# Opening order, state-pass buffers and the engine of the block differences in a hybrid convolution and mLSTM layer

## The chip, the core and the metric

The kernel runs on one core of a Trainium2 chip. The metric is device time in microseconds (us) of one execution. Engines are named as in the profile: PE (TensorE matmul), PEld (TensorE weight load), DVE (VectorE), ACT (ScalarE), POOL (GpSimd), SP (SyncE). SP issues nearly all DMA transfers, in order, so a transfer that has to wait holds those behind it.

## The reference, cut to what matters

One layer with 2048 latent tokens of 1024 channels and 256 context tokens, all in float32:

```python
shift, scale, gate = split(silu(c) @ w_ada + b_ada, 3)
hx = rmsnorm(x, g_norm) * (1 + scale) + shift           # 2048 x 1024
px = hx @ w_in + b_in                                    # 1024 -> 11296 columns
pc = hc @ w_in[:, :STATE_COLS] + b_in[:STATE_COLS]       # context: q, k, v and gates alone
_, ctx_states = mlstm_bidir(pc, (zero_state, zero_state), emit=False)
h_x, _ = mlstm_bidir(px[..., :STATE_COLS], ctx_states, emit=True)
y_a = b_a * dwconv3(c_a * x_a) * silu(z_a)
y_b = sigmoid(o) * headnorm(h_x) * silu(z_b)
merged = sigmoid(g_a) * (y_a @ w_pa) + sigmoid(g_b) * (y_b @ w_pb)
out = rmsnorm(x + gate * (merged @ w_out + b_out), g_final)
```

`mlstm_scan` steps over chunks of tokens. Each chunk's state is `C_new = decay * C + k^T (wk * v)`, together with a running sum n and a running maximum m. It is run forward and backward, from the final context state of that direction.

## The kernel before

**Matmuls.** Each float32 operand is split into a rounded part ("hi", a cast on ACT, L178) and a remainder ("lo", a subtraction on DVE, L179), and each product is three matmul passes (hi hi, hi lo, lo hi). The input projection works on pairs of 128-column blocks and two halves of 512 tokens with a scheme of seven block products in place of eight. `Stream` makes the seven weight operands from raw tiles. Their sums are formed on POOL (`total`, L345), and then split. `Operands` holds the seven token operands. PE's instructions run in the order in which the program writes them. The other engines' instructions are ordered by a scheduler, except those wrapped in `pin`, which keep program order on their engine.

**Halves.** The sequence is worked in two halves of 1024 tokens (`T`): A first, then B. Beside the dense matmuls, generators in two queues, `urgent` and `later`, put smaller work between PE's instructions. `run(dense, rate, urate)` takes a step of `later` after each 1/rate matmuls, and `gap(n)` is n steps of nothing.

**Opening.** The 1024 tokens of half A are loaded as eight tiles of 128 rows (`load_rows`), their squares are summed on ACT (L199), the scale is formed in three small steps on POOL (L200, L186, L187), and the rows are scaled on DVE (L205); together that is `norm`. The modulation vectors come from 16 tiles of `w_ada`, in four quarters kk of four tiles (`load_ada`). `ada(kk)` multiplies them on PE (L1045), `modulation(kk)` turns the result into `gsc` and `shift` on DVE (L1052 to L1054). `turned(kk, ns)` transposes four row tiles into a PSUM bank (L212) and applies the modulation (L216 on ACT, L217 on DVE). `cut_first` and `cut_sums` make the seven token operands of that quarter: differences on DVE (`less`, L1083), then the split. `mms(kk)` does the first four products of the quarter (L1062). The `w_ada` tiles lie in places that token operands take over later: the remainder tiles of the third quarter's operands 5 and 6 are those of the last modulation quarter.

**State pass.** The scan over chunks needs the state ahead of each chunk, in both directions. `state_scan` runs one direction in advance: for each pair of chunks it loads a tile of tokens (`tk`, from `tokd`, L702), weights v on POOL (`weigh`, vw, L631), multiplies k by it on PE (L636), updates the state on DVE (L640) and stores the states of both chunks back into `tokd` (L739). `load` runs one item ahead, with two `tk` buffers. `ctx_scan` does the same for the context. In half A it runs beside the dense products of `w_in`, in half B once for each pair of heads, between the dense products and the full `scan`, which uses the tags `tk`, `qk` and `mw` with two buffers each.

**Block differences.** While half A's products run, `prep_b` normalises and transposes half B's tokens into `xod`, and `late_rows` forms the gate row and multiplies `w_out` by it (L1295) into `wod`. `combine` then loads blocks of each and makes the four differences that the seven products need (L295), in place, and stores them. All these elementwise operations are on POOL. The input tiles are in a pool tag of four buffers (`big`).

Of the kernel before, what the change touches and what calls it, by code (L numbers as in the profile page):

```python
# [41 lines left out]
def hybrid_kernel(ctx: ExitStack, tc, x, c, ctxt, c_ctx, w_ada, b_ada, g_norm, w_in, b_in,  # L42
# [236 lines left out]
    def combine(src, tile):  # L279

        bs = {}

        def load(kk):
            if kk < 4:
                bs[kk] = [tile([P, 2, NB]) for _ in range(2)]
                for n, t in enumerate(bs[kk]):
                    ld.dma_start(t, src[2 * n:2 * n + 2, :, kk, :].rearrange("o p i -> p o i"))

        load(0)
        yield from gap(10)  # L290
        for kk in range(4):
            load(kk + 1)
            (b11, b12), (b21, b22) = [(t[:, 0, :], t[:, 1, :]) for t in bs[kk]]
            for d, a, b in ((b11, b12, b11), (b12, b22, b12), (b22, b22, b11), (b21, b21, b22)):
                pin(nc.gpsimd.tensor_tensor(d, a, b, op=OP.subtract))  # L295
                yield from gap(2)
            yield from gap(2)
            for n, t in enumerate(bs.pop(kk)):
                ld.dma_start(src[4 + 2 * n:6 + 2 * n, :, kk, :].rearrange("o p i -> p o i"), t)
            yield from gap(4)  # L300
# [352 lines left out]
        nc.scalar.copy(tok[:, :, 0:P], pt[:, 0:n * P].rearrange("p (c d) -> p c d", d=P))  # L653
        ld.dma_start(dst, tok)

    def tok_tile(pool):
        return pool.tile([P, 2, P + 258], F32, tag="tk", name=nm("tk"), bufs=2)

    def ctx_scan(pool):
        tks = {}  # L660

        def load(h):
            if h < NH:
                tks[h] = tok_tile(pool)
                ld.dma_start(tks[h][:, :, 0:P + 129], tcd[h])

        load(0)
        yield from gap(8)
        for h in range(NH):
            load(h + 1)  # L670
            tk = tks.pop(h)
            for d in (1, 0):
                g = gt["C"][d]
                order = (0, 1) if d == 0 else (1, 0)
                js = [h * 2 + c for c in order]
                vws = [weigh(tk[:, c], g["wk"][:, j:j + 1]) for c, j in zip(order, js)]
                yield from gap(2)
                mid, fin = cstate(), cstate()
                update(mid, None, tk[:, order[0]], vws[0], None, "pn")
                yield  # L680
                update(fin, mid, tk[:, order[1]], vws[1], g["dec"][:, js[1]:js[1] + 1], "pn")
                yield
                ld.dma_start(cini[h] if d == 0 else std[1][h], fin)

    def state_scan(pool, heads, half):

        d = 0 if half == 0 else 1
        g = gt["AB"[half]][d]
# [9 lines left out]
        def load(m):  # L698
            if m < len(items):
                h, p, _, c0 = spot(2 * m)  # L700
                tks[m] = tok_tile(pool)
                ld.dma_start(tks[m][:, :, 0:P + 129], tokd[half][h, :, c0:c0 + 2, 0:P + 129])  # L702
# [8 lines left out]
                vws[n] = weigh(tks[n // 2][:, ch - c0], g["wk"][:, j:j + 1])  # L711

        load(0)
        yield from gap(8)
        ready(0)
        yield from gap(2)
        for n in range(2 * len(items)):
            h, p, ch, c0 = spot(n)
            if n % 2 == 0:
                load(n // 2 + 1)  # L720
            else:
                yield
            tk = tks[n // 2]
# [287 lines left out]
              (1, 0), (1, 1), (0, 0), (0, 1), (5, 0), (5, 1), (6, 0), (6, 1)]  # L1011
    adas = {}

    def load_ada(kk):

        for n, m in enumerate((kk, kk + 4, NK + kk, NK + kk + 4)):
            o, p = PLACES[4 * kk + n]
            adas[kk, n] = xslot(4 * o + 2 * p + 1, [P, NK, P])
            ld.dma_start(adas[kk, n], w_ada.rearrange("(k p) n -> p k n", p=P)[:, :, m * P:(m + 1) * P])

    st = Stream((t[0] for t in todo), (0, 2, 1, 3, 4, 5, 6))
    load_rows(0, 4)
    load_ada(0)
    load_rows(4, 8)
    load_ada(1)
    st.begin()
    load_ada(2)
    load_ada(3)
# [8 lines left out]
    gsc = cp.tile([P, NK, 2], F32, name="gsc")  # L1037
    padas = {}

    def ada(kk):  # L1040

        pada = padas[kk] = pu_ps().rearrange("p (n a s) -> p n a s", n=4, s=2)
        for n in range(4):
            for k in range(NK):
                nc.tensor.matmul(pada[:, n], adas[kk, n][:, k, :], sc[:, k, None, :].to_broadcast([P, 64, 2]),  # L1045
                                 start=(k == 0), stop=(k == NK - 1))

    def modulation(kk):
# [13 lines left out]
            nc.tensor.matmul(ps[b], ops[o][wi][:, kk, :], xA.at(o, xi, kk), start=(not more and kk + pi == 0),  # L1062
                             stop=(kk == 3 and pi == 2), skip_group_check=True)

    def turned(kk, ns):

        for n in ns:
            pt = bank(n)
            turn(pt, rows[4 * (n // 2):4 * (n // 2) + 4], kk + 4 * (n % 2))
            v = vs[kk, n] = vslot() if n < 2 else t2k()  # L1070
            pin(modulate(v, pt, kk + 4 * (n % 2), 0, nc.scalar if n < 3 else None))

    def cut(kk, o, v):
        if kk % 2 == 0:
# [26 lines left out]
        for a in todo:  # L1101
            cut(*a)

    def mms(kk):
        for o, b in EARLY_OPS:
            mm(o, b, kk)

    EARLY_OPS = ((0, "X"), (2, "U"), (3, "W"), (1, "Y"))
    st.pinned = True
    ada(0)  # L1110
    normed(0, 4)
    transposed_rows()
    modulation(0)
    turned(0, (0, 1))
    cut_first(0)
    normed(4, 8)
    turned(0, (2, 3))
    ada(1)
    rest(cut_sums(0))
    modulation(1)  # L1120
    turned(1, range(4))
    cut_first(1)
    st.fill(2)
    more = cut_sums(1)
    st.fill(4)
# [2 lines left out]
    ps.update((b, dense_ps()) for _, b in EARLY_OPS)  # L1128
    ada(2)
    modulation(2)  # L1130
    turned(2, range(4))
    mms(0)
    cut_first(2)
    more = cut_sums(2)
    ada(3)
    modulation(3)
    rest(more)
    turned(3, range(4))
    mms(1)
    mms(2)  # L1140
    cut_first(3)
    rest(cut_sums(3))
    mms(3)
    s1, u2, u3 = uslot(), uslot(), uslot()
    nc.scalar.copy(s1, ps["X"])
    fin(0, 0, ps["U"], s1)
    nc.vector.tensor_tensor(u2, ps["Y"], s1, op=OP.add)
    nc.vector.tensor_tensor(u3, ps["W"], u2, op=OP.add)
    for n, (o, b) in enumerate(((4, "Z"), (5, "V"), (6, "Z"))):
        ops[o] = st.take(n + 1)  # L1150
        if o < 6:
# [95 lines left out]
    def late_rows():  # L1247
# [44 lines left out]
        for k in range(NK):  # L1292
            load(out_rows, k + 1)
            wr = wrs.pop(k)
            pin(nc.gpsimd.tensor_tensor(wr, wr, gate_t, op=OP.mult))  # L1295
# [4 lines left out]

    later.extend([prep_b(), late_rows()])
    later.append(ctx_scan(sb))
    later.append(state_scan(sb, range(NH), 0))
    for item, fin, w in todo[kv_end:]:
        run(pair(st, xA, fin), 0.235, 0.5)
    flush(urgent)
# [17 lines left out]
    EARLY = 3  # L1324
    kinds = half_fins(1)
    heads = [f"k{r} v{r} q{r} o{r} z{r} X{r} C{r} Z{r} B{r}" for r in range(4)]
    todo = plan(kinds, " ".join(heads) + " a0 a1 a2 a3 b0 b1 b2 b3")
    st = Stream(t[0] for t in todo)
    for item, fin, w in todo:
# [4 lines left out]
        if w[0] == "z":  # L1334
            flush(urgent)
            hs = 2 * r, 2 * r + 1
            later.extend([state_scan(sp_, hs, 1), scan(sp_, hs, 1)])
            if r < EARLY:
                later.append(scan(sp_, [r], 0))
    flush(urgent)  # L1340
# [204 lines left out]
```

## Time and profile before

| | |
|---|---|
| time, median of 3 runs | 2711.37 us (2708.78 to 2716.03) |
| the profiled execution | 2719.64 us, span 2717.9 us |
| PE busy | 2613.6 us, 96% of the span |
| DVE, ACT, POOL busy | 1717.8, 1063.4, 1216.7 us |
| mean granted TensorE clock | 0.988 |
| DMA | 458.10 MB, mean 169 GB/s |

A row of the timeline has the start, the duration, the engine, the source line, the operation, output <- input by tile names, partitions x elements, and a count; the bracket is the idle time of the engine ahead of it and what ended that. "SPq" rows are the DMA issues. In lists of waits the columns are total, number of times and longest. In tables of stretches the columns are the stretch, its length, the busy time of PE, PEld, DVE, ACT and POOL with their instruction counts, then the granted clock, the mean busy share of the DMA engines, and GB/s.

### The profile page before, as it was taken

What the parts mean: (1) busy time and instruction counts of PE and PEld (TensorE: products, weight loads), DVE (VectorE), ACT (ScalarE), POOL (GpSimd) and SP (SyncE); (2) the same over time, 40 slices, a digit from 0 to 9 for tenths busy, and PEclk for the clock granted to TensorE, in tenths of its full rate; (3) what the DMA queues carried; (4) which work ended last, traced back from release to release, by engine and by line L of the source; (5) the groups of instructions that cost most, each with busy time, mean ns of one, the idle gap of its engine ahead of it and who ended that gap; (6) DMA issues with size and microseconds to landing.
All of it is one profiled execution on the core that took longest, in us unless ns stands there. A gap on an engine that the chain in (4) does not pass through costs nothing.

```text
span 2717.9 us, 38189 instructions
## 1 busy us (share of the span) xinstructions
PE 2613.6 (96%) x12807; PEld 2176.6 (80%) x12807; DVE 1717.8 (63%) x3075; ACT 1063.4 (39%) x2168; POOL 1216.7 (45%) x1411
## 2 busy tenths in 40 slices
PE   5999999999999999999999999999999999899998
PEld 5788887787778787877887888788888888788776
DVE  4642338888876657477577577667656655444686
ACT  4433334333343335343443444344444433222332
POOL 2212123544665543235555565465555335433464
PEclk8999999999999999999999999999999999999999
DMA  7323343555633567434644654654556978868542
GB/s 218 92 93 106 104 138 119 176 162 159 213 124 103 171 180 240 118 104 144 196 151 122 183 165 133 180 172 126 168 180 211 301 246 258 267 196 280 201 147 93
DMA packets 370082, 458.10 MB, mean 169 GB/s; under 512 B 23853, under 2 KB 268253, under 8 KB 369885
## 3 DMA queue, kind: packets, MB, share of 16 engines
q1 hardware_dynamic: 369648, 455.57, 54.3%
q8 instruction: 102, 1.67, 0.3%
q14 instruction: 96, 0.78, 0.1%
q10 hardware_dynamic: 236, 0.08, 0.0%
HBM read 324.60 MB, written 130.97 MB: 168 GB/s over the span
## 4 chain that ended last, share of the span: by engine, by line
PE 62%; DVE 7%; DMA 5%; issue 3%; POOL 2%; ACT 1%; SPq 0%; POOLq 0%; DVEq 0%; ACTq 0%
PE pd L412 43%; PE pd L459 11%; PE pn L841 2%; PE pn L842 2%; DVE wl L179 2%; DMA tokd<-tk 1%; PE pn L636 1%; DMA tk<-tokd 1%; PE pa L793 1%; PE pu L636 1%; DVE xt L1467 1%; DVE cv L946 1%; DMA x<-xod 1%; DVE t2k L873 1%; DMA xt<-in_x_dram 1%
## 5 line engine op out<-in xcount | busy, mean ns | idle before, releaser
L412 PE MATMUL pd<-x,wh 128*128 128x512 f32 x5320 | 1702.5, 398 | 27.9 <-DVE t2k L873 14.7
L412 PEld LDWEIGHTS pd<-x,wh 128*128 128x128 f32 x5320 | 988.9, 190 | 224.7 <-issue 28.6
L412 PE MATMUL pd<-x,wl 128*128 128x512 f32 x2660 | 1060.9, 399 | 0.0
L412 PEld LDWEIGHTS pd<-x,wl 128*128 128x128 f32 x2660 | 503.8, 189 | 100.2 <-issue 0.2
L179 DVE TENSOR_TENSOR wl<-sw,wh 128x512 fp32r<-128x512 f32 x384 | 314.1, 819 | 195.1 <-ACT wh L178 188.8
L178 ACT CAST wh<-sw 128x512 fp32r<-128x512 f32 x384 | 238.2, 620 | 504.4 <-PE pd L412 426.8
L178 ACT CAST wh<-wr 128x512 fp32r<-128x512 f32 x352 | 217.8, 619 | 403.6 <-PE pd L412 260.4
L179 DVE TENSOR_TENSOR wl<-wr,wh 128x512 fp32r<-128x512 f32 x352 | 299.3, 851 | 44.3 <-ACT wh L178 43.4
L345 POOL TENSOR_TENSOR sw<-wr,sw 128x512 f32<-128x512 f32 x96 | 134.0, 1396 | 395.4 <-DVE wl L179 327.7
L631 POOL TENSOR_SCALAR vw<-tk,wk 128x129 f32<-128x129 f32 x272 | 200.0, 743 | 209.4 <-DMA tk<-tokd 153.5
L459 PE MATMUL pd<-x,wh 128*128 128x512 f32 x896 | 283.1, 398 | 0.0
L345 POOL TENSOR_TENSOR sw<-wr 128x512 f32<-128x512 f32 x96 | 130.2, 1356 | 196.6 <-DVE wl L179 187.1
L459 PEld LDWEIGHTS pd<-x,wh 128*128 128x128 f32 x896 | 167.3, 189 | 32.5
L459 PE MATMUL pd<-x,wl 128*128 128x512 f32 x448 | 174.4, 399 | 0.0
L345 POOL TENSOR_TENSOR sw<-sw,wr 128x512 f32<-128x512 f32 x96 | 135.3, 1409 | 74.5 <-DVE wl L179 62.9
L854 ACT ACTIVATE hf<-pn,rd 128x128 f32<-128x128 f32 x128 | 47.0, 368 | 275.1 <-DVE rd L850 256.5
L779 POOL TENSOR_SCALAR_AFFINE_SELECT mw<-mw 128x256 f32<-128x256 f32 x128 | 64.3, 523 | 200.2 <-DMA mw<-mwd 168.3
L873 DVE TENSOR_TENSOR t2k<-pd,u 128x512 f32<-128x512 f32 x168 | 115.4, 687 | 59.4 <-PE pd L412 58.6
L345 POOL TENSOR_TENSOR sw<-wr,wr 128x512 f32<-128x512 f32 x96 | 137.4, 1431 | 18.5 <-DMA wr<-in_w_in_dram 12.4
L186 POOL TENSOR_SCALAR ssq<-ssq 128x1 f32<-128x1 f32 x128 | 36.9, 288 | 186.5 <-ACT hf L856 180.6
L841 PE MATMUL pn<-tk,pt 128*128 128x129 f32 x512 | 99.5, 276 | 3.1 <-DVE hb L855 3.1
L880 DVE SCALAR_TENSOR_TENSOR t2k<-pd,cols,u 128x512 f32<-128x512 f32 x73 | 54.7, 750 | 74.0 <-PE pd L412 68.0
(236 smaller groups left out, 3331.6 us busy)
## 6 DMA issues: line engine op xcount, KB each, us to landing
wr<-in_w_in_dram SPq DMA_DIRECT2D x176, 512.0 KB, 4.2
mw<-mwd SPq DMA_DIRECT2D x64, 512.0 KB, 5.1
tk<-tokd SPq DMA_DIRECT2D x64, 386.0 KB, 4.2
tk<-tokd SPq DMA_DIRECT2D x64, 257.0 KB, 3.0
qkd<-t2k SPq DMA_DIRECT2D x64, 256.0 KB, 2.9
qk<-qkd SPq DMA_DIRECT2D x64, 256.0 KB, 3.9
tokd<-t2k SPq DMA_DIRECT2D x32, 258.0 KB, 3.0
tokd<-tk SPq DMA_DIRECT2D x64, 129.0 KB, 3.4
```

What stands on the lines that cost most here:

```text
L178: a = nc.scalar.copy(hi, raw)
L179: b = (eng or nc.vector).tensor_tensor(lo, raw, hi.bitcast(F32), op=OP.subtract)
L345: nc.gpsimd.tensor_tensor(s, a, b, op=op)
L412: nc.tensor.matmul(ps[b], op[wi][:, kk, :], xs.at(o, xi, kk), start=(fresh and kk + pi == 0), stop=(o == last[b] and kk == 3 and pi == 2), ...
L459: nc.tensor.matmul(pss[j], ops[k // 4][wi][:, k % 4, :], y(xi, k, j), start=(k + pi == 0), stop=(k == NK - 1 and pi == 2))
L631: pin(nc.gpsimd.tensor_scalar(vw, tk[:, VT], wk, None, op0=OP.mult))
L636: nc.tensor.matmul(pu, tk[:, KT], vw, start=True, stop=True)
L779: pin(nc.gpsimd.affine_select(mws[m][:, :, 0, d, :], mws[m][:, :, 0, d, :], pattern=[[0, 2], [s, P]], base=0, channel_multiplier=-s, compa ...
L841: nc.tensor.matmul(pn[:, d, :], pt[:, d, :], tk[:, VT], start=True, stop=False)
L842: nc.tensor.matmul(pn[:, d, :], qw[:, d, :], cur if d == carried else tk[:, ST], start=False, stop=True)
L873: nc.vector.tensor_tensor(t, ps, add, op=OP.add)
L880: nc.vector.scalar_tensor_tensor(dst, ps, bcol(col), add, op0=OP.add, op1=OP.add)
```

## The change

1. Loads: the first modulation quarter comes ahead of all x rows; the second quarter's first two tiles come between the two groups of four rows, and its other two behind them.
2. Opening order: the first two modulation tiles are multiplied ahead of everything else; the squares and scaling of rows 4 and 5 move ahead of the first transposes' modulation, those of rows 6 and 7 behind the first split. The modulation of the first two transposed tiles is done on DVE, all others on ACT. From the second quarter on, parts of the early products and of the transposes alternate; `rest(more)` of the third quarter comes ahead of the last `modulation`; the fifth operator's weights are taken ahead of the first evacuation.
3. State pass: four buffers in place of two, loads two items ahead. In half B the odd items use the `mw` buffers. The context pass gets four buffers.
4. The differences in `combine` and the product of `w_out` with the gate are on DVE.

```diff
@@ combine
-                pin(nc.gpsimd.tensor_tensor(d, a, b, op=OP.subtract))
+                pin(nc.vector.tensor_tensor(d, a, b, op=OP.subtract))
@@ late_rows
-            pin(nc.gpsimd.tensor_tensor(wr, wr, gate_t, op=OP.mult))
+            pin(nc.vector.tensor_tensor(wr, wr, gate_t, op=OP.mult))
@@ state pass
-    def tok_tile(pool):
-        return pool.tile([P, 2, P + 258], F32, tag="tk", name=nm("tk"), bufs=2)
+    def tok_tile(pool, bufs=2):
+        return pool.tile([P, 2, P + 258], F32, tag="tk", name=nm("tk"), bufs=bufs)
...
-                tks[h] = tok_tile(pool)
+                tks[h] = tok_tile(pool, 4)
...
-                tks[m] = tok_tile(pool)
+                tks[m] = tok(m)
...
         load(0)
+        load(1)
         yield from gap(8)
...
-                load(n // 2 + 1)
+                load(n // 2 + 2)
...
-    later.append(state_scan(sb, range(NH), 0))
+    later.append(state_scan(sb, range(NH), 0, lambda m: tok_tile(sb, 4)))
...
+    def tok_b(m):
+        if m % 2 == 0:
+            return tok_tile(sp_)
+        t = sp_.tile([P, NK, P], F32, tag="mw", name=nm("tm"), bufs=2)
+        return t.rearrange("p k n -> p (k n)")[:, 0:2 * (P + 258)].rearrange("p (c n) -> p c n", c=2)
...
-            later.extend([state_scan(sp_, hs, 1), scan(sp_, hs, 1)])
+            later.extend([state_scan(sp_, hs, 1, tok_b), scan(sp_, hs, 1)])
@@ loads
+    load_ada(0)
     load_rows(0, 4)
-    load_ada(0)
+    load_ada(1, (0, 1))
     load_rows(4, 8)
-    load_ada(1)
+    load_ada(1, (2, 3))
@@ turned
-            pin(modulate(v, pt, kk + 4 * (n % 2), 0, nc.scalar if n < 3 else None))
+            pin(modulate(v, pt, kk + 4 * (n % 2), 0, eng))      # eng=nc.scalar by default
@@ opening
-    ada(0)
+    ada(0, (0, 1))
+    transposed_rows()
     normed(0, 4)
-    transposed_rows()
+    ada(0, (2, 3))
     modulation(0)
-    turned(0, (0, 1))
+    normed(4, 6)
+    turned(0, (0, 1), None)
     cut_first(0)
-    normed(4, 8)
+    normed(6, 8)
+    ada(1, (0, 1))
     turned(0, (2, 3))
-    ada(1)
+    ada(1, (2, 3))
     rest(cut_sums(0))
     modulation(1)
-    turned(1, range(4))
+    turned(1, (0, 1))
     cut_first(1)
+    turned(1, (2, 3))
     st.fill(2)
...
     ada(2)
     modulation(2)
-    turned(2, range(4))
-    mms(0)
+    mms(0, (0, 1))
+    turned(2, (0, 1))
     cut_first(2)
+    mms(0, (2, 3))
+    turned(2, (2, 3))
     more = cut_sums(2)
     ada(3)
+    rest(more)
     modulation(3)
-    rest(more)
-    turned(3, range(4))
-    mms(1)
+    mms(1, (0, 1))
+    turned(3, (0, 1))
+    cut_first(3)
+    mms(1, (2, 3))
+    turned(3, (2, 3))
     mms(2)
-    cut_first(3)
     rest(cut_sums(3))
     mms(3)
     s1, u2, u3 = uslot(), uslot(), uslot()
     nc.scalar.copy(s1, ps["X"])
+    ops[4] = st.take(0)
     fin(0, 0, ps["U"], s1)
...
+    st.fill(1)
     for n, (o, b) in enumerate(((4, "Z"), (5, "V"), (6, "Z"))):
-        ops[o] = st.take(n + 1)
+        if n:
+            ops[o] = st.take(n)
```

More of the change, by code (lines that the diff above doesn't have):

```diff
@@ L683, in ctx_scan, with state_scan @@
                 ld.dma_start(cini[h] if d == 0 else std[1][h], fin)
-    def state_scan(pool, heads, half):
+    def state_scan(pool, heads, half, tok):
         d = 0 if half == 0 else 1
@@ L1012, in hybrid_kernel, with load_ada @@
     adas = {}
-    def load_ada(kk):
-        for n, m in enumerate((kk, kk + 4, NK + kk, NK + kk + 4)):
+    def load_ada(kk, ns=range(4)):
+        for n in ns:
+            m = (kk, kk + 4, NK + kk, NK + kk + 4)[n]
             o, p = PLACES[4 * kk + n]
@@ L1038, in hybrid_kernel, with ada @@
     padas = {}
-    def ada(kk):
-        pada = padas[kk] = pu_ps().rearrange("p (n a s) -> p n a s", n=4, s=2)
-        for n in range(4):
+    def ada(kk, ns=range(4)):
+        if kk not in padas:
+            padas[kk] = pu_ps().rearrange("p (n a s) -> p n a s", n=4, s=2)
+        for n in ns:
             for k in range(NK):
-                nc.tensor.matmul(pada[:, n], adas[kk, n][:, k, :], sc[:, k, None, :].to_broadcast([P, 64, 2]),
+                nc.tensor.matmul(padas[kk][:, n], adas[kk, n][:, k, :], sc[:, k, None, :].to_broadcast([P, 64, 2]),
                                  start=(k == 0), stop=(k == NK - 1))
@@ L1063, in mm, with turned @@
                              stop=(kk == 3 and pi == 2), skip_group_check=True)
-    def turned(kk, ns):
+    def turned(kk, ns, eng=nc.scalar):
         for n in ns:
@@ L1102, in rest, with mms @@
             cut(*a)
-    def mms(kk):
-        for o, b in EARLY_OPS:
+    EARLY_OPS = ((0, "X"), (2, "U"), (3, "W"), (1, "Y"))
+    def mms(kk, ns=range(4)):
+        for n in ns:
+            o, b = EARLY_OPS[n]
             mm(o, b, kk)
-    EARLY_OPS = ((0, "X"), (2, "U"), (3, "W"), (1, "Y"))
     st.pinned = True
-    ada(0)
+    ada(0, (0, 1))
+    transposed_rows()
     normed(0, 4)
-    transposed_rows()
+    ada(0, (2, 3))
     modulation(0)
-    turned(0, (0, 1))
+    normed(4, 6)
+    turned(0, (0, 1), None)
     cut_first(0)
-    normed(4, 8)
+    normed(6, 8)
+    ada(1, (0, 1))
     turned(0, (2, 3))
-    ada(1)
+    ada(1, (2, 3))
     rest(cut_sums(0))
     modulation(1)
-    turned(1, range(4))
+    turned(1, (0, 1))
     cut_first(1)
+    turned(1, (2, 3))
     st.fill(2)
```

## The prediction

> **What bounds the kernel now.** I read the page's busy shares first, then the list of PE's waits, then a table of the opening by stages, then the timelines of single engines at the places which that list names.
>
> ```profile
> PE 2613.6 (96%) x12807; PEld 2176.6 (80%) x12807; DVE 1717.8 (63%) x3075; ACT 1063.4 (39%) x2168; POOL 1216.7 (45%) x1411
> ```
>
> PE is busy for 2613.6 of 2717.9 us, and the change takes no matmul away. All that can be won is PE's 104 us of idle time and the time that it ran at a reduced clock. PE's order is written by hand, so each wait delays everything behind it. The largest waits (line, releaser: sum, times, longest):
>
> ```profile
> PE pd L412 <- DVE t2k L873: 14.7, 7, 5.0
> PE pn L636 <- POOL vw L631: 11.8, 11, 2.2
> PE pu L1045 <- DMA x<-in_w_ada_dram: 10.1, 1, 10.1
> PE pt L212 <- DVE xr L205: 10.0, 4, 5.7
> ```
>
> Each part of the change faces one group. The opening has the third and fourth rows, the state pass has the second (vw is what L631 makes from a loaded token tile), and the first lies mostly where POOL does the block differences.
>
> ```profile
> 16.00:36.00 20.00, 10.07 (x67) 8.68 (x65) 6.06 (x14) 7.38 (x20) 6.33 (x14) 0.82 1.14 329
> ...
> 57.00:88.00 31.00, 25.09 (x140) 21.61 (x141) 22.09 (x42) 15.34 (x26) 3.95 (x3) 0.89 0.08 26
> ```
>
> The columns are stretch, length, busy time of PE, PEld, DVE, ACT, POOL, then granted clock, DMA share, GB/s. From 16 to 36 us the DMA engines are full (1.14). From 57 to 88 us DMA is almost idle (0.08) and PE still misses 5.9 us, at a clock of 0.89: that stage is held by engine order, not by data.
>
> **The opening.** The modulation is made in quarters, and its third step (L1052 to L1054 on DVE) is the best clock of the opening.
>
> ```profile
> 13.32 9.95 PE L1045 MATMUL pu<-sc,x 128*128 128x128 f32 x64 [10.14 <-DMA x<-in_w_ada_dram]
> 60.73 1.11 PE L212 MATMUL pt<-ident,xr 128*128 128x128 f32 x4 [4.32 <-ACT cv L216]
> 67.11 7.31 PE L1045 MATMUL pu<-sc,x 128*128 128x128 f32 x64
> 87.47 0.50 PE L1062 MATMUL pd<-x,wl 128*128 128x512 f32 x1 [1.66 <-DVE wl L179]
> 27.38 0.63 ACT L199 ACTIVATE t2k<-xr 128x512 f32<-128x512 f32 x1
> 29.93 0.75 DVE L205 TENSOR_SCALAR xr<-xr,rs 128x1024 f32<-128x1024 f32 x1 [1.64 <-POOL rs L187]
> 31.68 0.75 DVE L205 TENSOR_SCALAR xr<-xr,rs 128x1024 f32<-128x1024 f32 x1 [1.00 <-POOL rs L187]
> 34.62 1.74 DVE L205 TENSOR_SCALAR xr<-xr,rs 128x1024 f32<-128x1024 f32 x1 [0.71 <-POOL rs L187]
> 37.79 0.81 DVE L217 TENSOR_SCALAR t2k<-pa,gsc,shift 128x512 f32<-128x512 f32 x1 [1.42 <-PE pa L212]
> 38.51 0.76 DVE L1083 TENSOR_TENSOR u<-t2k,cv 128x512 f32<-128x512 f32 x1
> 43.75 0.69 DVE L179 TENSOR_TENSOR x<-t2k,x 128x512 fp32r<-128x512 f32 x1
> 45.67 0.16 DVE L1052 SCALAR_TENSOR_TENSOR gsc<-pu,cols 128x4 f32<-128x4 f32 x1 [1.24 <-PE pu L1045]
> 58.59 0.16 DVE L1052 SCALAR_TENSOR_TENSOR gsc<-pu,cols 128x4 f32<-128x4 f32 x1
> 74.45 0.16 DVE L1052 SCALAR_TENSOR_TENSOR gsc<-pu,cols 128x4 f32<-128x4 f32 x1 [5.32 <-PE pu L1045]
> 1.58 4.22 SPq L1007 DMA_DIRECT2D xr<-in_x_dram  x4
> 5.84 7.07 SPq L1019 DMA_DIRECT2D x<-in_w_ada_dram  x4
> 12.96 3.13 SPq L1007 DMA_DIRECT2D xr<-in_x_dram  x4
> 16.13 9.10 SPq L1019 DMA_DIRECT2D x<-in_w_ada_dram  x4
> DMA to landing us min/median/max: 3.7/5.9/8.0
> ```
>
> (The last row is the landing time of the x rows.) The sixteen loads stay the same and the DMA engines are full, so their last one lands when it did; only the order inside changes. With the same issue costs (7.07 us for four weights, 3.13 for four rows, half of 9.10 for two weights) SP issues the first quarter from 1.6 to 8.7 us, rows 0 to 3 to 11.8, half the second quarter to 16.3, rows 4 to 7 to 19.5. Row 3 lands at about 17.5 us, row 5 near 24 (issued near 17.9, 5.9 later). The first weights land between 3.7 us after issue, like a row in idle engines, and 7.5, as now (13.32 - 5.84). So PE starts the modulation between 5.3 and 9.1 instead of at 13.3 us, but that wins nothing by itself: the scaled rows now come later. From square to the end of scaling takes 3.3 us (27.38 to 29.93 + 0.75), so row 5 is done near 27.3, and since DVE keeps program order, the first modulation of tokens, moved to DVE, stands behind it: two times 0.81, to 28.9; then casts and remainders, to 30. The squares of rows 6 and 7 follow the casts on ACT from 29.9; the second of a pair is scaled 31.68 + 0.75 - 27.38 = 5.05 us after the first square starts, at 35.0, against 36.4 before (34.62 + 1.74). The fourth modulation moves from DVE to ACT, which takes 0.8 off the path to the first difference (38.51). So the chain that ends at 45.67 ends 2.2 us sooner; I take 2, from 0 (rows 5 and 7 land 2 us later, 8.0 in place of 5.9) to 4 (they land at 3.7).
>
> Second to third quarter (45.67 to 58.59, 12.9 us) keeps the same DVE work in the same order: 0.
>
> Third to fourth quarter is 74.45 - 58.59 = 15.9 us now, because PE waits 4.32 us for the third modulation, then transposes, then runs twelve matmuls, then the last 7.31 us of modulation matmuls. After the change the first matmuls and transposes stand ahead of that wait, so the last quarter's matmuls need only the transposes behind ACT's first result: 0.3 us for the modulation step, 0.8 for ACT's first result, 1.1 for four transposes (the 60.73 row) and 0.2 between them, so 2.4 us after 58.59's event, then 7.31, ending at 9.7. DVE's chain on the other side is about 3.9 us from modulation to first difference (four modulations of 0.8 on ACT, 0.7 between) and 43.75 + 0.69 - 38.51 = 5.9 behind it: 9.8. The remainders in `rest(more)` now stand ahead of the modulation on DVE, and the last of them waits for the end of the modulation matmuls, since it overwrites their weights: + 0.7. That makes 10.4: a gain of 5.5 (2 to 6).
>
> Behind the fourth quarter the chain of differences is as long as before: 0. The wait of 1.66 at 87.47 shrinks as operator 4's weights are split ahead of the first evacuation: 0.9. Opening: 2 + 5.5 + 0.9 = 8.4, range 2 to 11.
>
> **State pass.**
>
> ```profile
> SPq L702 <- DMA tokd<-tk: 102.2, 48, 4.3
> 1480.60 0.36 SPq L739 DMA_DIRECT2D tokd<-tk  x1
> 1485.31 0.36 SPq L702 DMA_DIRECT2D tk<-tokd  x1
> 1488.36 1.20 POOL L631 TENSOR_SCALAR vw<-tk,wk 128x129 f32<-128x129 f32 x2 [3.60 <-DMA tk<-tokd]
> 1455.00:1502.00 47.00, 40.63 (x180) 31.82 (x179) 34.14 (x59) 13.46 (x21) 22.10 (x24) 0.96 0.48 134
> ```
>
> With two buffers a load waits on SP until the store out of its buffer has landed: issued at 1480.60, the load goes 4.7 us later, and POOL waits for it. That held SP 48 times, 102.2 us, with every other DMA behind it. With four buffers the load reuses a buffer whose store went out an item earlier, and has two items' time. PE's waits for vw are 11.8 us; not all lie at loads alone, so I take three quarters, 8.8. The clock in the pass shown is 0.96 over 40.6 busy us, 1.6 us lost; the three others are shorter in waits, and I take 1.7 for all four. State pass: 10.5, from 3 (SP's other waits hold the loads) to 18 (all waits, and 1.6 in each pass). The odd tiles now take the `mw` buffers that the scan behind uses; its first loads take those of items 4 and 5, whose stores went out two items earlier: 0. The context scan has four buffers but loads one ahead, and its PE waits name DVE: 0.
>
> **Differences on DVE.** Thirty-two operations of 128x512 and eight of 128x1024 (the gate times w_out) leave POOL.
>
> ```profile
> 500.00:785.00 285.00, 273.83 (x1181) 223.47 (x1180) 236.31 (x263) 104.07 (x165) 161.88 (x98) 0.98 0.56 177
> 688.13 5.64 POOL L1295 TENSOR_TENSOR xb<-xb,xb 128x1024 f32<-128x1024 f32 x2
> 685.07 0.74 DVE L948 SCALAR_TENSOR_TENSOR cv<-cv,cols,cv 128x504 f32<-128x504 f32 x1
> 688.74 2.76 DVE L948 SCALAR_TENSOR_TENSOR cv<-cv,cols,cv 128x504 f32<-128x504 f32 x1
> L1272 DVE SCALAR_TENSOR_TENSOR acc<-xb,sc,acc x7: 1270/1279/2308, 589.0 to 624.6; 128x1024 f32<-128x1024 f32 x7
> 509.87 1.32 POOL L295 TENSOR_TENSOR xb<-xb,xb 128x512 f32<-128x512 f32 x1 [2.43 <-DMA xb<-xod]
> 700.00:720.00 20.00, 17.12 (x65) 13.96 (x66) 17.80 (x22) 8.45 (x13) 10.58 (x7) 0.83 0.68 212
> ```
>
> On DVE they cost 32 x 0.69 + 8 x 1.28 = 32.3 us. Against that stands what POOL did to DVE: the same L948 takes 0.74 us alone and 2.76 beside two L1295, 2.0 longer. If each L1295 (2.82 us) stretches its DVE neighbours by 1.5 to 2.0 and an L295 of 1.32 us, at the same rate, by 0.7, DVE gets 12 to 16 + 22 back. So DVE's load stays level, and POOL is free for the weight sums sooner. [...]
>
> Of the waits on L873 the longest, 5.0 us, ends in a backlog of DVE with some four L1295 in it; half a microsecond each is 2, and the clock, 0.83 in 700 to 720, cost 2.9 there, of which I take half. Against these stands 2.43 us that POOL waited for the first blocks and DVE now may, with evacuations queued behind it: half, 1.2. Net gain 2; ends -32 (nothing comes back and all of it is PE's) and +8 (that wait and its clock loss go).
>
> **Sum.** 8.4 + 10.5 + 2 = 21. The profiled execution took 2719.6 us (span 2717.9); 2698.6 for it. It stood 8.3 us above the median of 2711.4, and the forecast for the median is 2690.
>
> **Rivals.** First, the rows are late: the opening's first part is no sooner and the third saves its low end, 2 + 0.9 in place of 8.4. For it: DMA share 1.14 from 16 to 36 us. Against it: from 57 us there is no DMA to wait for. 2711.4 - 2.9 - 12.5 = 2696.
>
> Second, slower: DVE becomes the bound from 500 to 785 us. Place: the differences stand ahead of PSUM evacuations on DVE, which is busy 236.3 of 285 already. Price: 32.3 us if no stretch returns, all as PE waits: 2711.4 - 18.9 + 32.3 = 2725. It loses to before from 18.9 us of new waits on, and shows as slower from 27. For it: four of the L873 waits lie here. Against it: the stretched rows.
>
> Third, the buffers do nothing: loads still late, since SP takes them in order behind other waits; the context and first passes never waited much. 2711.4 - 8.4 - 2 - 0.5 = 2700. With late rows too: 2706, within the noise.
>
> Fourth, all waits go: 11 + 18 + 8 gives 2674.
>
> **Chances.** Forecast 0.50 (its own range 2682 to 2698), rows late 0.14, buffers nothing 0.10, both 0.09, everything 0.08, DVE the bound 0.09. A measurement here tells 0.3%, or 8 us, from no change: below 2703 count the forecast, all waits gone, rows late and most of the third, 0.79; slower gets 0.08. The range 2674 to 2708 leaves out the slower rival and the tails.
>
> **What the profile would show.** Right: fourth L1052 near 66 us in place of 74.5; PE's vw waits under 4 us and few SP waits of L702 on tokd stores; DVE's busy time from 500 to 785 within 10 us of 236, L873's waits not above 15. Wrong: DVE idle on xb loads, L873's waits doubled, or the first L1052 behind row 7.

## The result, and the profile after

The changed kernel takes 2686.4 us (median of 4 runs, 2685.7 to 2688.9) against 2710.9 us for the kernel before: a ratio of 0.9909, 95% interval 0.9891 to 0.9926. A second series of the same kernel gave 0.9922 (0.9907 to 0.9936). The forecast was 2690. The profiled execution of the changed kernel took 2685.8 us, with a span of 2684.0.

The line of busy times of the page, after:

```profile
PE 2601.9 (97%) x12807; PEld 2171.1 (81%) x12807; DVE 1725.5 (64%) x3113; ACT 1063.1 (40%) x2170; POOL 1149.8 (43%) x1371
```

The 12807 matmuls are the same. PE's idle time is span less busy: 104.3 us before, 82.1 after. So 22.2 of the 33.9 us between the two spans were idle time, and 11.7 are less busy time of the same matmuls, at a mean granted clock of 0.991 in place of 0.988. In a second pair of traces (below) the spans differ by 26.8 us, of which 22.9 are idle time and 3.9 busy time (clocks 0.991 and 0.989): the idle time repeats, the share of the busy time does not. From PE's list of waits after (line, releaser: sum, times, longest):

```profile
PE pd L412 <- DVE t2k L874: 11.0, 5, 3.5
PE pt L212 <- DVE xr L205: 9.3, 6, 4.1
PE pu L636 <- POOL vw L631: 6.7, 2, 5.2
...
PE pt L212 <- ACT cv L216: 4.3, 2, 2.5
...
PE pn L636 <- POOL vw L631: 3.4, 3, 1.7
```

L874 was L873 before, and L1049 was L1045. The wait of 10.1 us for the first modulation weights is gone (3.0 for another input is left), vw fell from 11.8 to 3.4, and L874 from 14.7 to 11.0. The matmul into `pu` of the full scan waits for vw too, a row that the prediction's list does not show: 8.1 us before, 6.7 after.

I cut both traces at the same matmuls, so that each stage holds the same work of PE, and took the length and PE's idle time of each stage. The second column of each kernel is another execution of it; the pairs show what is repeatable.

| stage, length / PE idle (us) | before | before, 2nd | after | after, 2nd |
|---|---|---|---|---|
| opening, to the first L412 | 95.3 / 30.7 | 94.8 / 30.5 | 86.0 / 20.9 | 85.9 / 20.9 |
| from there to the last context product (L439) | 293.4 / 1.4 | 293.4 / 1.4 | 293.4 / 1.4 | 293.4 / 1.4 |
| from there to the first L636 (holds the differences) | 405.8 / 13.9 | 404.8 / 14.0 | 399.4 / 10.8 | 402.4 / 10.8 |
| from the first to the 33rd pair of L636 (context) | 87.9 / 3.5 | 87.9 / 3.5 | 87.9 / 3.5 | 87.9 / 3.5 |
| half A's state pass, up to half B's | 332.4 / 8.8 | 332.3 / 10.1 | 328.3 / 6.6 | 329.4 / 6.5 |
| half B's four state passes together | 138.8 / 13.5 | 136.2 / 12.6 | 126.5 / 6.8 | 126.5 / 6.8 |
| between those passes | 631.3 / 3.1 | 633.8 / 4.1 | 633.0 / 4.7 | 631.4 / 4.7 |
| the rest, up to PE's last matmul | 724.5 / 21.2 | 722.6 / 21.2 | 721.2 / 19.4 | 722.2 / 20.0 |

Idle times repeat within 1.3 us, mostly within 0.3. Lengths repeat less well (405.8 and 404.8, 399.4 and 402.4), and the difference lies in PE's busy time: 391.9 and 390.8 us, both at a granted clock of 0.99, and 388.6 at 1.00 and 391.6 at 0.99. An update of the state is a pair of L636 matmuls, and 8.4 us of each span lie behind the last matmul. The opening with the old order reaches its first dense product between 93.6 and 95.8 us in the six traces that have it, the new one between 85.9 and 86.1 in four.

The opening after, in single rows: DVE's second to fourth modulation step, and PE at the waits of which the text speaks. The step L1056 was L1052 before, and the wait at 78.08 was that at 87.47. The last row is PE's first dense product in the kernel before, the one ahead of it the same after.

```profile
5.98 5.22 PE L1049 MATMUL pu<-sc,x 128*128 128x128 f32 x32 [2.96 <-DVE sc L174]
42.47 0.15 DVE L1056 SCALAR_TENSOR_TENSOR gsc<-pu,cols 128x4 f32<-128x4 f32 x1
55.63 0.16 DVE L1056 SCALAR_TENSOR_TENSOR gsc<-pu,cols 128x4 f32<-128x4 f32 x1
57.79 0.66 PE L212 MATMUL pt<-ident,xr 128*128 128x128 f32 x4 [1.80 <-ACT cv L216]
58.72 7.31 PE L1049 MATMUL pu<-sc,x 128*128 128x128 f32 x64
66.12 0.69 DVE L179 TENSOR_TENSOR x<-t2k,x 128x512 fp32r<-128x512 f32 x1 [0.68 <-PE pu L1049]
66.73 0.15 DVE L1056 SCALAR_TENSOR_TENSOR gsc<-pu,cols 128x4 f32<-128x4 f32 x1
78.08 0.50 PE L1066 MATMUL pd<-x,wl 128*128 128x512 f32 x1 [1.26 <-DVE wl L179]
85.96 0.62 PE L412 MATMUL pd<-x,wh 128*128 128x512 f32 x2
95.30 0.62 PE L412 MATMUL pd<-x,wh 128*128 128x512 f32 x2
```

The last modulation matmuls start at 58.72 in place of 67.11. The remainder at 66.12 waits 0.68 us for their end, as it overwrites their weights, and the fourth step follows. From 57 to 88 us PE now does 28.9 us of work in place of 25.1, at a clock of 1.00 in place of 0.89:

```profile
57.00:88.00 31.00, 28.90 (x169) 24.79 (x170) 23.31 (x42) 17.93 (x30) 4.18 (x4) 1.00 0.24 77
```

The state pass. SP's waits of L702 after, then what POOL waited for at vw, after and before:

```profile
SPq L702 <- DMA tokd<-tk: 62.9, 31, 4.3
SPq L702 <- DMA tokd<-tm: 12.5, 7, 2.8
POOL vw L631 <- DMA tk<-tokd: 27.2, 13, 6.1
POOL vw L631 <- DMA tk<-tokd: 153.5, 56, 7.5
```

SP still stands 38 times, 75.4 us in all, at a load that has to wait for a store (48 times and 102.2 us before). But POOL's waits for loaded tokens fell from 153.5 us to 27.2 (and 1.2 for tm): the loads are early enough now, although they wait as before.

### The profile page after: what moved, and what is told of

It is laid out like the page before. It is cut to its first block, busy times and chain, and to the rows that moved or that the text cites. A ratio compares the mean times of both kernels' runs of the same rounds, so it can differ in the third digit from the quotient of the medians.

```text
span 2684.0 us, 38156 instructions
## 1 busy us (share of the span) xinstructions
PE 2601.9 (97%) x12807; PEld 2171.1 (81%) x12807; DVE 1725.5 (64%) x3113; ACT 1063.1 (40%) x2170; POOL 1149.8 (43%) x1371
## 3 DMA queue, kind: packets, MB, share of 16 engines
q8 instruction: 102, 1.67, 0.3%
## 4 chain that ended last, share of the span: by engine, by line
PE 82%; DVE 8%; issue 3%; POOL 2%; DMA 2%; ACT 2%; SPq 0%; POOLq 0%; ACTq 0%; DVEq 0%
PE pd L412 58%; PE pd L459 11%; PE pn L842 2%; PE pn L843 2%; PE pc L439 2%; DVE wl L179 2%; PE pn L636 1%; PE pa L647 1%; PE pa L794 1%; PE pu L636 1%; DVE cv L947 1%; PE pd L492 1%; DVE t2k L874 1%; PE pa L809 0%; DVE cv L949 0%
## 5 line engine op out<-in xcount | busy, mean ns | idle before, releaser
L412 PE MATMUL pd<-x,wh 128*128 128x512 f32 x5320 | 1697.0, 397 | 22.4 <-DVE t2k L874 11.0
L412 PEld LDWEIGHTS pd<-x,wh 128*128 128x128 f32 x5320 | 986.0, 189 | 216.9 <-issue 23.2
L412 PE MATMUL pd<-x,wl 128*128 128x512 f32 x2660 | 1058.1, 398 | 0.5 <-DVE wl L179 0.5
L412 PEld LDWEIGHTS pd<-x,wl 128*128 128x128 f32 x2660 | 501.9, 189 | 100.4 <-DVE wl L179 0.9
L179 DVE TENSOR_TENSOR wl<-sw,wh 128x512 fp32r<-128x512 f32 x384 | 316.2, 825 | 189.5 <-ACT wh L178 183.0
L178 ACT CAST wh<-sw 128x512 fp32r<-128x512 f32 x384 | 237.8, 620 | 491.8 <-PE pd L412 405.4
L179 DVE TENSOR_TENSOR wl<-wr,wh 128x512 fp32r<-128x512 f32 x352 | 280.8, 798 | 43.2 <-ACT wh L178 41.9
L631 POOL TENSOR_SCALAR vw<-tk,wk 128x129 f32<-128x129 f32 x240 | 179.8, 753 | 151.6 <-PE pn L636 117.8
L459 PEld LDWEIGHTS pd<-x,wh 128*128 128x128 f32 x896 | 167.0, 189 | 32.3
L874 DVE TENSOR_TENSOR t2k<-pd,u 128x512 f32<-128x512 f32 x168 | 115.5, 687 | 59.9 <-PE pd L412 58.5
L345 POOL TENSOR_TENSOR sw<-wr,wr 128x512 f32<-128x512 f32 x96 | 136.2, 1419 | 17.7 <-DMA wr<-in_w_in_dram 7.7
```

The source lines that it names most:

```text
L178: a = nc.scalar.copy(hi, raw)
L179: b = (eng or nc.vector).tensor_tensor(lo, raw, hi.bitcast(F32), op=OP.subtract)
L345: nc.gpsimd.tensor_tensor(s, a, b, op=op)
L412: nc.tensor.matmul(ps[b], op[wi][:, kk, :], xs.at(o, xi, kk), start=(fresh and kk + pi == 0), stop=(o == last[b] and kk == 3 and pi == 2), ...
L459: nc.tensor.matmul(pss[j], ops[k // 4][wi][:, k % 4, :], y(xi, k, j), start=(k + pi == 0), stop=(k == NK - 1 and pi == 2))
L631: pin(nc.gpsimd.tensor_scalar(vw, tk[:, VT], wk, None, op0=OP.mult))
```

## Experiments

In the first group each part of the change was put alone into the kernel before.

**The opening alone** (the hunks `loads`, `turned` and `opening`):

> The new opening alone; state pass and differences as before. Theory (the three parts add): the four modulation steps on DVE at 42.5, 55.6 and 66.7 us (second to fourth) as in the changed kernel, dense products from 86 us on in place of 95.3, no other wait of PE changed, so 9.3 us less: 2702. Rival (the opening's lead is eaten later, where PE waits for DVE or for loads that are no sooner): the lead at 100 us is 9.3 but below 5 at the end, 2706 or more.

Measured: ratio 0.997 (0.9957 to 0.9983), first dense product at 86.1 us. The whole gain of the opening, 8.7 or 9.2 us against the two traces of before, is there without the other parts.

**The first half of the opening alone** (loads, squares, first quarter; the third quarter and what follows as before):

```diff
+    load_ada(0)
     load_rows(0, 4)
-    load_ada(0)
+    load_ada(1, (0, 1))
...
+    normed(4, 6)
-    turned(0, (0, 1))
+    turned(0, (0, 1), None)
     cut_first(0)
-    normed(4, 8)
+    normed(6, 8)
...
```

> The opening's first half alone: order of loads, modulation first, squares ahead, up to the second quarter; from the third quarter on the order of before. Theory: the second modulation step at 42.5 in place of 45.67 and then the old distances (12.9 and 15.9), so the fourth near 71.3 and 3.2 us less in all: 2708. Rival: the loads are what counts, and the first half carries most of the 9.3: 2704 or less.

Measured: 1.000 (0.9989 to 1.0011). Its first dense product starts at 91.7 us, 3.2 to 3.6 us sooner than in the two traces of before (94.8 and 95.3), but the time does not show it: the interval reaches to a gain of 3 us and no further. Its second step is at 42.4 us, as in the whole change, and the fourth follows the third by 14.8 us, as in most kernels with the old order.

**The second half of the opening alone** (from `mms(0, (0, 1))` on, with the fifth operator's weights):

```diff
-    turned(2, range(4))
-    mms(0)
+    mms(0, (0, 1))
+    turned(2, (0, 1))
     cut_first(2)
+    mms(0, (2, 3))
+    turned(2, (2, 3))
     more = cut_sums(2)
     ada(3)
+    rest(more)
     modulation(3)
-    rest(more)
...
```

> The opening's second half alone: products and transposes in turns from the third quarter on, rest(more) ahead of the last modulation, the fifth operator's weights ahead of the first evacuation; loads and first two quarters as before. Theory (order on PE and DVE, not data): the third modulation step stays at 58.6, the fourth comes 11 us behind it, near 69.7 in place of 74.5, and dense products start 5.5 to 6 us sooner: 2704 to 2706. Rival (the two halves need each other): without the earlier loads and squares the second half waits elsewhere, and dense products start less than 3 us sooner.

Measured: 0.9967 (0.9952 to 0.9981), first dense product at 88.0 us, about 7 us sooner. Some 2 us of these are not its own: its second step is at 44.0 us, and up to there the kernel is the one before, where that step lies between 45.1 and 47.3 in the six other traces. Its own are the steps behind: third to fourth 11.1 us in place of 15.9 or 14.8 (the two traces of before), and 0.9 behind the fourth. So the matmuls and transposes put ahead of the third modulation's wait carry 5 to 6 us, more than half of the opening.

**The state pass alone** (four buffers, loads two items ahead):

> The state pass alone: four buffers, loads two ahead, in all three places. Theory: PE's waits for vw in the state passes fall from 11.8 to under 4 us and the step into half B (1060 to 1085 us) loses some 2 of its 5.3 us of waits, since SP no longer carries late loads; 10 to 16 us less: 2695 to 2701. Rival (SP order): the loads are early in the program but late on SP; vw waits stay above 8 and the gain is under 5: 2706 or more. Second rival: the gain of half B comes with the differences on DVE, since POOL is freer, and this kernel gains only 6.

Measured: 0.9974 (0.9961 to 0.9987), 7 us (4 to 11), short of the 10 to 16 expected, though PE's waits for vw fell to 1.7 us as the theory had it.

**Four buffers, but loads one item ahead as before** (against the kernel with the state pass alone):

```diff
         load(0)
-        load(1)
         yield from gap(8)
...
-                load(n // 2 + 2)
+                load(n // 2 + 1)
```

> Of the state pass only the four buffers, with loads one item ahead as before. Theory of the buffers (the load waits for the store out of its buffer, and that is all): SP's waits of the loads for stores go away, and PE's vw waits fall to 3 or less, as with loads two ahead: 2703. Rival (distance): what helps is that the load is issued an item earlier; one ahead leaves the 3 us of landing on the path, vw waits stay at 5 or more, and the gain is under half of the state pass's 7 us: 2707 or more.

Measured: 0.9957 (0.9943 to 0.997): the buffers alone give no less than buffers and distance together. PE's waits for vw, and then the second of half B's state passes cut at the same matmuls, here and before (31.9 us in the whole change too):

```profile
PE pn L636 <- POOL vw L631: 1.7, 2, 0.9
```

```profile
1456.90:1488.81 31.91, 29.73 (x141) 23.43 (x140) 26.55 (x50) 10.88 (x17) 19.27 (x19) 1.00 0.56 161
```

```profile
1458.33:1496.76 38.43, 32.06 (x141) 24.72 (x140) 27.37 (x50) 10.88 (x17) 17.45 (x19) 0.96 0.49 132
```

With four buffers this pass takes 31.9 to 32.3 us in every kernel that has them; with two it took 33.3 to 38.4. The idle time in it was 3.2 to 6.4 us with two (6.4 and 5.2 in the traces of before) and is 2.2 to 2.5 with four. SP is not free by it: it still waits 37 times for a store here, 70.5 us in all.

But this pair of kernels does not test the distance. SP's order is not pinned, and the 64 loads L702 and 64 stores stand in it in the same order in both. Half A begins with four loads, and then a store and a load go by turns; with two buffers it begins with two. So a load stands directly behind the store out of its own buffer, whatever distance the program asks for, and the number of buffers sets how many items ahead that is: three in place of one. The start of half B's first pass, here and with loads two ahead:

```profile
1215.33 0.37 SPq L739 DMA_DIRECT2D tokd<-tk  x1
...
1217.57 0.36 SPq L702 DMA_DIRECT2D tk<-tokd  x1
1219.14 0.36 SPq L739 DMA_DIRECT2D tokd<-tm  x1
```

```profile
1214.16 0.37 SPq L740 DMA_DIRECT2D tokd<-tk  x1
...
1216.40 0.36 SPq L702 DMA_DIRECT2D tk<-tokd  x1
1217.98 0.36 SPq L740 DMA_DIRECT2D tokd<-tm  x1
```

**Differences and gate product on DVE alone:**

```diff
-                pin(nc.gpsimd.tensor_tensor(d, a, b, op=OP.subtract))
+                pin(nc.vector.tensor_tensor(d, a, b, op=OP.subtract))
...
-            pin(nc.gpsimd.tensor_tensor(wr, wr, gate_t, op=OP.mult))
+            pin(nc.vector.tensor_tensor(wr, wr, gate_t, op=OP.mult))
```

> The differences and the gate product on DVE alone. Theory: DVE's stretch beside POOL returns about what the moved operations cost, DVE's busy time from 500 to 781 us goes from 234.6 to about 241, and the waits on the evacuation at 678 and 703 us shrink from 6.4 to 3.5; 4 to 7 us less: 2704 to 2707. Rival: DVE is level and PE does not gain, 2709 to 2713, and what the changed kernel gained between 470 and 780 us came from the earlier opening. Second rival: DVE waits for the blocks loaded from DRAM; 2715 or more, with idle time of DVE named by xb loads.

Measured: 0.9985 (0.9976 to 0.9995), 4 us (1 to 7). The waits of 6.4 us at 678 and 703 us are one of 3.5 here, as expected.

**The gate product alone on DVE** (the second of these two lines, differences on POOL):

> Only the product of w_out with the gate (eight operations of 128x1024) goes to DVE; the 32 differences stay on POOL. Theory: the long operations stretch DVE most for what they do, so the waits on the evacuation at 678 and 703 us go from 6.4 to about 3.5 here too, and the lead between 650 and 795 us is 4 us or more: 2706. Rival: the 32 differences carry it, and the lead there is under 2 us: 2709.

Measured: 0.9982 (0.9971 to 0.9992), as much as both lines. Two waits of PE tell why. Before, PE waited here twice for an evacuation (first fence); with the gate product on DVE (second fence) the first of these waits is gone and the other is 1.5 us shorter:

```profile
678.51 0.70 PE L412 MATMUL pd<-x,wh 128*128 128x512 f32 x2 [1.38 <-DVE t2k L873]
...
702.88 1.19 PE L412 MATMUL pd<-x,wh 128*128 128x512 f32 x2 [5.04 <-DVE t2k L873]
```

```profile
699.07 1.19 PE L412 MATMUL pd<-x,wh 128*128 128x512 f32 x2 [3.56 <-DVE t2k L873]
```

The kernels with differences and gate product on DVE show 3.53 us at this place and no other wait there; the kernels without (opening alone, state pass alone, both together) show 1.36 or 1.37 and 5.06 to 5.08. In idle time, the table's 13.9 against 10.8, the gate product carries 2.7 (it alone leaves 11.2) and the differences 0.4.

**All but the DVE part** (opening and state pass together):

> The opening and the state pass together, differences and gate product on POOL. If the changed kernel's 3.5 us between the two halves come from the differences being on DVE (in company with the state pass), this stretch is 153.5 to 155 here; if from opening and state pass together, 150 to 151. The stretch of the differences is 292 (286.4 with all three parts). Sum of the single parts: opening 0.997, state pass 0.9974, so 0.9944 and about 2696; rival (the parts help one another so that the differences on DVE alone give nothing more): 0.991, 2687.

Measured: 0.9948 (0.9933 to 0.9963), 2695.3 us. The stretch up to the first L636 takes 405.4 us, as before. The single parts add up, as the first expectation had it (0.997 and 0.9974 make 0.9944). The DVE part is worth 6.7 us on top of these two (2695.3 against 2688.6), 0.9985 by itself; in PE's idle time it is 3.0 (85.6 against 82.6).

**The whole change once more**, for what repeats:

> The changed kernel once more. If the 3.5 us that it gained between the end of the first half's state pass and the second half's first state pass (150.3 us there, 153.7 to 155.2 in every kernel with one part of the change alone) come from the change, the second profile shows 150 to 151 there again; if they are chance of one execution, 153.5 to 155. Opening up to the first dense product 85.5 to 86.5, four state passes of the second half 126 to 128 in all. Time 2686, ratio 0.991.

Measured: 0.9922 (0.9907 to 0.9936). The stretch from the end of half A's state pass to half B's first takes 150.9 us again, and 150.5 without the DVE part, so the differences are not its cause. But with all three parts and another opening (the next experiment) it takes 153.6. Its two halves without the DVE part, and with the other opening:

```profile
1050.39:1125.62 75.23, 73.56 (x342) 59.69 (x343) 40.07 (x60) 33.57 (x53) 16.20 (x16) 1.00 0.60 183
1125.62:1200.84 75.22, 73.60 (x329) 59.28 (x328) 52.33 (x123) 31.31 (x61) 22.51 (x19) 1.00 0.29 90
```

```profile
1046.27:1123.09 76.82, 75.93 (x342) 61.95 (x343) 39.67 (x60) 33.94 (x53) 16.08 (x16) 0.96 0.59 178
1123.09:1199.91 76.82, 75.20 (x328) 60.42 (x327) 52.79 (x123) 31.46 (x61) 21.96 (x19) 0.98 0.28 89
```

PE's idle time in the two is 3.3 and 2.5 us (2.6 in the second trace of the change); the longer one has the less. What differs is the granted clock (0.96 and 0.98 against 1.00), which makes 151.1 us of busy time out of 147.2. So neither expectation holds for all kernels: the step from 150.5 to 153.6 is the clock's and belongs to no part. What is left for the change in this stretch is 2 to 3 us of idle time (6.0 in the first trace of before); which part takes them away stays open, since the state pass alone (2.4) and all three (3.2 and 2.6) have them and the buffers with loads one ahead (5.2), the opening alone (4.9) or the DVE part alone (4.7) do not.

**First modulation back on ACT, ahead of the squares.** The trace after shows DVE's order at the first step: row 5's scaling stands ahead of the first modulation of tokens. To see whether that bounds the opening:

```diff
-    normed(4, 6)
-    turned(0, (0, 1), None)
+    turned(0, (0, 1))
     cut_first(0)
-    normed(6, 8)
+    normed(4, 8)
```

> The changed kernel with the first two modulations of tokens back on ACT, ahead of the squares of rows 4 to 7, so that they don't stand behind the scaling of row 5 on DVE. Theory (the first step of the opening is held by DVE's program order): the second modulation step moves from 42.5 to about 39.5 us, the steps behind it follow by the same amount, the first dense product starts at 83 in place of 86, time about 3 us less than the changed kernel (2683). Rival (the rows and the second quarter's weights land too late to be of use, or the later squares put the scaling of rows 4 to 7 back by as much): step two within 1 us of 42.5, time as the changed kernel.

Measured: 0.9925 (0.991 to 0.9941) of before, no gain over the change (0.9922 in the same series). The second step is at 41.5 us, 0.9 sooner, not 3. The first difference (L1087) starts 2.3 us sooner, at 32.65 in place of 34.91, but the sums on POOL start when their weights land, as they did, and one instruction of DVE more now takes some 1.7 us in place of 0.68 beside them:

```profile
33.50 1.54 DVE L1087 TENSOR_TENSOR u<-t2k,t2k 128x512 f32<-128x512 f32 x1 [0.16 <-ACT t2k L216]
34.96 1.76 DVE L179 TENSOR_TENSOR x<-u,x 128x512 fp32r<-128x512 f32 x1
36.65 1.75 DVE L1087 TENSOR_TENSOR cv<-t2k,u 128x512 f32<-128x512 f32 x1
...
33.22 1.27 POOL L345 TENSOR_TENSOR sw<-wr,wr 128x512 f32<-128x512 f32 x1 [2.71 <-DMA wr<-in_w_in_dram]
```

Behind that, PE is the bound. Its wait for the second step is 4.58 us long instead of 2.46, and behind it the granted clock is 0.65 from 45 to 50 us, where the change has 1.00. PE here, then in the change:

```profile
42.77 1.12 PE L212 MATMUL pt<-ident,xr 128*128 128x128 f32 x4 [4.58 <-ACT cv L216]
...
44.54 9.22 PE L1049 MATMUL pu<-sc,x 128*128 128x128 f32 x64
```

```profile
44.09 0.66 PE L212 MATMUL pt<-ident,xr 128*128 128x128 f32 x4 [2.46 <-ACT cv L216]
...
45.02 7.31 PE L1049 MATMUL pu<-sc,x 128*128 128x128 f32 x64
```

The 64 matmuls take 9.22 us in place of 7.31, and from 54 to 68 us PE is not idle at all. The first dense product starts at 85.3, 0.6 us sooner. In the opening's idle time the gain is 2.0 us (18.9 against 20.9), and PE's busy time, 66.4 us against 65.0, takes 1.4 of it back. The lower clock is not this order's alone: the second trace of the change has a wait of 3.56 us, a clock of 0.75 from 45 to 50 us and 8.13 us for the 64 matmuls at this place.

**With that, the third fill directly behind the second step:**

```diff
+    st.fill(2)
     turned(1, (0, 1))
     cut_first(1)
     turned(1, (2, 3))
-    st.fill(2)
```

> As the kernel before it in this list, with the weight splits of the third fill moved to directly behind the second modulation step, where DVE was idle for 2.4 us. Theory: another 2.4 us, third step near 50 and fourth near 61.5, first dense product at 80 to 81, time about 5 us less than the changed kernel (2681). Rival (the third quarter's modulation weights, landing at 41 to 49 us, hold PE there, or the split delays the first differences on DVE): third step no sooner than in the kernel without this move, time the same as that one.

Measured: 0.9926 (0.991 to 0.9941), the same again. The third step comes at 52.6 us (54.3 without this move, 55.6 in the change) and the fourth at 64.9, so the move does what it says, 1.8 us; it ends where PE's modulation matmuls end, and the first dense product starts at 84.1, 1.9 us sooner than in the change. A gain of that size (2.2 us in idle time) is below what these intervals tell. No version beat the changed kernel.

## Why the prediction was right, point by point

**Opening, 8.4 forecast, 9.3 in the trace.** By the steps: second modulation 3.2 us sooner (2 taken), second to third 13.2 in place of 12.9 (0 taken), third to fourth 11.1 in place of 15.9, so 4.8 (5.5 taken), and behind the fourth 1.6 (0.9 taken). In the second pair of traces it is 3.9, 13.2 in place of 12.9, 3.7 and 1.6. The fourth step is at 66.7, forecast "near 66". The path was the one forecast, but the sizes on it erred both ways, so that the sum came so near is in part luck:

- To the second step, the last row was scaled at 33.5 us in place of the 35.0 worked out, since the rows were there sooner. The first two differences then took 1.58 and 1.75 us beside POOL's sums instead of 0.7 each, which gave part of it back.
- From the third step to the fourth, the step itself was put at 0.3 us. It takes 1.2, and did before (58.59 to 59.81 us, its last instruction 1.03). So the modulation matmuls start 3.1 us behind the step, not 2.4, and end at 10.4, not 9.7. The last remainder does wait for them, and the fourth step stands 0.7 us behind their end, as forecast. Also, 15.9 was the longer of two values for this stretch: it is 14.8 in the second trace of before.
- Behind the fourth step, operator 4's weight split does go ahead of the additions of the evacuation. But the wait that was to shrink by 0.9 shrank by 0.4, from 1.66 to 1.26, as PE reaches it 1.3 us sooner after the step.

In measured time the opening alone gives 0.30% of 2710.9, 8 us (5 to 12).

**State pass, 10.5 forecast.** In the stages half B's four passes are 9.7 or 12.3 us shorter, by which trace of before one takes; 5.8 or 6.7 of that is idle time, and 0.5 to 1.6 us more idle time stands between the passes. Passes and what lies between them together had 16.6 and 16.7 us of idle time before and have 11.4 in both traces after: 5.2 us less. Half A's idle time went from 8.8 and 10.1 to 6.6 and 6.5, but there the pass alone and the buffers alone show 6.5 and 8.4 and the opening alone 6.7, so I can't give it to the state pass. The context lost nothing, as forecast. In time: 0.9957 and 0.9974, so 7 to 12 us. The sum was right, but its terms were not, and that is luck. PE's waits for vw fell by 8.4 us (8.8 taken), of which 5.2 is idle time won in half B. PE's busy time in the four passes fell by 3.9 or 5.6 us (1.7 taken, for the clock): the granted clock was 0.95, 0.96 or 0.99, 1.00 and 1.00 before and is 1.00 in all four after, but with the state pass alone the first of them is at 0.95 still.

Two steps were wrong. "Few SP waits of L702 on tokd stores" failed: 38 are left. And the load does not have "two items' time" behind a store that "went out an item earlier": on SP it still stands directly behind the store out of its own buffer and waits for it. It is only the load for four items on instead of two, and so early enough for POOL.

**Differences on DVE, net 2 forecast.** Idle time of PE fell by 3.1 us, and the measured worth is 4 us alone and 6.7 with the rest. Right: DVE's load stays level. From the last context product to the first L636, after and then before:

```profile
379.35:778.76 399.41, 388.61 (x1732) 318.21 (x1731) 323.90 (x417) 155.62 (x264) 133.17 (x109) 1.00 0.52 168
```

```profile
388.72:794.53 405.81, 391.86 (x1733) 320.07 (x1731) 320.83 (x377) 156.15 (x264) 204.79 (x149) 0.99 0.52 163
```

DVE's busy time grew by 3.1 us, although the moved operations (L295 in two forms, and L1312, which was L1295) cost 17.4 + 11.9 + 13.0 = 42.3 us there. The weight splits (L179, from two kinds of input) gave 131.2 - 111.8 = 19.4 us of that back, and other operations of DVE the rest. After and then before:

```profile
L179 DVE TENSOR_TENSOR wl<-sw,wh 128x512 fp32r<-128x512 f32 x79 | 66.8, 849 | 21.4 <-ACT wh L178 16.5 <-PE pa L647 2.1 <-PE pa L1255 1.8
L179 DVE TENSOR_TENSOR wl<-wr,wh 128x512 fp32r<-128x512 f32 x59 | 45.0, 763 | 1.3 <-ACT wh L178 1.2
...
L295 DVE TENSOR_TENSOR xb<-xb 128x512 f32<-128x512 f32 x16 | 17.4, 1088 | 0.0
...
L1312 DVE TENSOR_TENSOR xb<-xb,xb 128x1024 f32<-128x1024 f32 x8 | 13.0, 1628 | 0.0
...
L295 DVE TENSOR_TENSOR xb<-xb,xb 128x512 f32<-128x512 f32 x16 | 11.9, 746 | 0.2
```

```profile
L179 DVE TENSOR_TENSOR wl<-sw,wh 128x512 fp32r<-128x512 f32 x79 | 73.7, 936 | 24.7 <-ACT wh L178 19.9 <-PE pa L647 2.1 <-PE pa L1238 1.8
L179 DVE TENSOR_TENSOR wl<-wr,wh 128x512 fp32r<-128x512 f32 x59 | 57.5, 974 | 1.2 <-ACT wh L178 1.2
```

The moved operations are stretched in their turn: 16 of the differences took 1088 ns on average where 690 were taken, and POOL has only its sums and normalisations left. A difference with POOL idle takes 0.68 to 0.69 us; seven of the 32 took 1.67 to 1.79, and three of the eight products 2.31 in place of 1.22, each with an operation of POOL at the same time; six more differences took 0.68 or 0.69 although a sum of POOL ran for some 0.5 us of each. The stretching cost 10 us of DVE's time (42.3 against 32.3), and no idle time of PE shows for it. The term that was too small is the waits: besides the shorter wait (1.5 us, forecast "half a microsecond each is 2") a second wait of 1.4 us went; the stretch itself is 2.4 or 6.4 us shorter by the two pairs of the table, and what goes beyond 3.1 is busy time of PE (391.9 to 388.6 us in the two stretches shown above, at a granted clock of 0.99 and 1.00). The 1.2 us set against it, DVE waiting for its first blocks, did not appear.

**Sum.** 21 forecast; 24.5 and 21.4 in the two series. Each part won in the place that was named; terms of 1 to 4 us erred in both directions and came out even.

## What to carry to other kernels

When a load waits for the store out of its own buffer, look first at the order on the queue: here a load already stood directly behind that store, and more buffers moved it forward, while an earlier place in the program did not. Look for success in the consumer's wait, not the queue's. In a chain that crosses four engines, the cheap gain was to put finished work ahead of the wait (5 to 6 us here); where PE had no idle time left (54 to 68 us), moving steps of DVE or ACT forward gained no time (0.9925 and 0.9926 against 0.9922). Cut two traces at the same matmuls and compare idle times, since these mostly repeat to 0.3 us here (1.3 at worst), where a stage length differs by 3 us (399.4 at a clock of 1.00 and 402.4 at 0.99).

## What the runs showed of the hardware that I had not expected

Behind one and the same wait of PE the matmuls ran at the full granted clock in one execution and at half of it in another. The two traces of the changed kernel have the same wait, 3.53 us, at the same matmul. In the first the two matmuls behind it take 0.70 us, and the granted clock is 1.00 from 690 to 695 us; in the second they take 1.19 us, and it is 0.50:

```profile
689.87 0.70 PE L412 MATMUL pd<-x,wh 128*128 128x512 f32 x2 [3.53 <-DVE t2k L874]
...
690.00:695.00 5.00, 5.00 (x23) 4.10 (x24) 4.65 (x8) 3.58 (x6) 0.00 (x0) 1.00 0.91 291
```

```profile
690.05 1.19 PE L412 MATMUL pd<-x,wh 128*128 128x512 f32 x2 [3.53 <-DVE t2k L874]
...
690.00:695.00 5.00, 4.95 (x12) 3.92 (x13) 4.65 (x7) 3.24 (x5) 0.00 (x0) 0.50 0.87 305
```

In these 5 us PE runs 23 matmuls in the first and 12 in the second. The kernel is the same in both, so the change does not settle which of the two an execution gets. The waits ahead of the same operation in the kernel before stand on either side: behind 1.38 us the two matmuls take 0.70 (clock 1.00 from 679 to 684 us), behind 5.04 they take 1.19 (0.50 from 703 to 708).

Busy time differs between executions in the whole as well: the same 12807 matmuls took 2613.6 and 2608.8 us in the two traces of before (mean granted clock 0.988 and 0.989), 2601.9 and 2604.9 in those of after (0.991 in both). That is why a single profile can't tell 4 us, and why the first profile of the change looked 3.5 us better than the second.
